# One line of weight loads up to attention, compression chunks in turn with projections, values earlier, taps spread wider

## The chip, the cores and the metric

The kernel runs on one core of a Trainium2 chip. The metric is the device time of one execution in microseconds; the median of several runs is compared.

## What is computed

One layer of a decoder trunk over x of 1024 rows by 1024 columns. All projections of one RMS-normalised input come from one weight matrix: a convolution group (256 channels, gated, causal depthwise filter of 31 taps, LayerNorm, swish) and an attention group (12 query heads, 4 key and value heads of 64) with three branches: compressed blocks, selected blocks and a window. The compressed keys and values come from a small network over windows of 32 rows:

```python
def compress(kr, pe, w1, w2):
    b, t = kr.shape[:2]
    chunks = kr.reshape(b, t // CMP_STRIDE, CMP_STRIDE, N_KV_HEADS, HEAD_DIM)
    lo = jnp.einsum("bclgd,ldh->bcgh", chunks, w1[:CMP_STRIDE])
    hi = jnp.einsum("bclgd,ldh->bcgh", chunks, w1[CMP_STRIDE:])
    h = lo[:, :-1] + hi[:, 1:] + jnp.einsum("ld,ldh->h", pe, w1)
    return jnp.einsum("bngh,hd->bngd", jax.nn.silu(h), w2)
```

The branches are gated and summed, joined with the convolution group, projected out and added to x; a SwiGLU network and a last RMSNorm follow.

## The kernel before

Every product is made of three passes: weights and data are each split into a high part (rounded for the fast matmul type) and a low remainder, and hi·hi, hi·lo and lo·hi are summed in PSUM. A weight chunk therefore costs a load and a split. `load_w` (L214) does it: SP starts the DMA into `w_raw` (two buffers), ACT casts `w_hi` (L225), and POOL subtracts `w_lo` in four pieces (L229), or DVE in one piece where `eng=dve` is given.

```python
raw = wp.tile([P, WCH], F32, tag="raw", name="w_raw", bufs=2)
act.copy(hi[:, :n], raw[:, :n])
step = n // PIECES if eng is pool else n
eng.tensor_sub(lo[:, q], raw[:, q], hi[:, q].bitcast(F32))
```

`w_hi` and `w_lo` have three buffers each. A `Feed` (L193) holds a list of loads and issues each one two ahead of the chunk that is being fetched.

The rows of x are worked on in two halves of 512. The first stretch, up to attention, is written as generators that a `Drive` (L149) runs one after the other on PE: the convolution's input (`conv_in`), the key's rows for the compression (`compress_in`, tiles `zc`, split into `xh` on ACT and `xl` on DVE by L233), the first two query projections (`project_d`, tiles `zo`), the key compression (`compress`: four chunks of w1, 24 matmuls each, into the two banks `h0` and `h1`, then swish, `af` at L475, split `ah`, `al`, and the second matrix in `compress_k`), four more query projections, the window's values (`values`, tiles `vo`), the value's `compress_in`, one window-key and one selected-key projection, the value compression, the two other key projections with `compress_v` (tiles `dup`, `vc`) before the last. Each yields the time it is meant to take; `Drive` adds these up, and side generators that are due are stepped in between: `late_rows` (the second half's rows), `tables`, `taps_in` (the depthwise filter, one DVE instruction per tap, L553), four stages of the compressed branch's scores (`stages_in`: `sc`, `cs`, `pg`, `pt`, `pct`, with an exponential at L623 on ACT), and `conv_tail` (LayerNorm and swish of the filter's result, L567 to L590: `cl`, `cn`, `cm`, `cf`, `m`, then a DMA to `mix_d`). After that, attention takes over, filled by the second half's projections (`fill_b`), whose first is a query projection. A scheduler then fixes the order on each engine; an engine works strictly in that order. In the kernel before, the w1 chunks are loaded inside `compress`, with `w_lo` on DVE, and each group of projections has a feed of its own.

Of the kernel before, what the change touches and what calls it, by code (L numbers as in the profile page):

```python
# [19 lines left out]
P = 128  # L20
# [21 lines left out]
C_KC = C_Q + HEADS * HD  # L42
C_VC = C_KC + 256
# [3 lines left out]
C_VW = C_KW + 256  # L47
# [41 lines left out]
def tile_hymba(ctx: ExitStack, tc, x, attn_norm, w_in, conv_w, conv_b, conv_ln_g, conv_ln_b,  # L89
# [186 lines left out]
    def win_chunk(c0):  # L276
        return load_w([(0, w_in[0, :, c0:c0 + P])], KT, P)
# [66 lines left out]
    def late_rows():  # L344
        for t in range(4, 8):
            with tc.issue_after(rows_in[0].ins), tc.issue_after(rows_in[1].ins):
                late[:] = [norm_rows(xts[t], xts[t], grow, pa, a4("junk"))]
            yield 2.4
            transpose_tile(xts[t], hhi[1], hlo[1], (t % 4) * P)

    rows = a4("rows")[:, :P]
# [76 lines left out]
            for i, z in ((0, zh), (1, zl)):  # L428
                sp.dma_start(dst[i, row:row + P, hf * 512:(hf + 1) * 512], z.bitcast(F32))

    def compress_in(ws, pe_col, out):
        xh = pa.tile([P, 8, GROUPS, 68], F32R, tag="xc", name="xh", bufs=2)
        xl = pa.tile([P, 8, GROUPS, 68], F32R, tag="xc", name="xl", bufs=2)
        for X in (xh, xl):
# [14 lines left out]
                        split(dh, dl, src)  # L449
        out.extend((xh, xl))  # L450

    def compress(xh, xl, w1, w2, tag, out):
        w1f = w1[0].rearrange("l d h -> (l d) h")
        hs = [bank("h0", tag), bank("h1", tag)]
        n = 0
        for jc in range(4):
            wh, wl = load_w([(0, w1f[jc * 512:(jc + 1) * 512, :])], 4, 256, dve)
            if jc == 1:
                w2r = pa.tile([P, 2, HD], F32, tag="w2r", name="w2r")
                pool.tensor_copy(w2r[:, 0, 0:1], wh[:, 0, 0:1].bitcast(F32))  # L460
            for j4 in range(4):
                j, s = (jc * 4 + j4) % 8, jc // 2
                for a, b in ((wh, xh), (wl, xh), (wh, xl)):
                    for ht in range(2):
                        mm(hs[ht][:, :264], a[:, j4, ht * P:(ht + 1) * P], b[:, j, :, s:s + 66],
                           start=n < 2, stop=n >= 94)
                        n += 1
                        yield 0.12
# [391 lines left out]
    def q_load(m):  # L860
        return lambda: win_chunk(C_Q + m * P)
# [16 lines left out]
    def taps_in(n):  # L878
        taps = conv_taps(0)
        for _ in taps:  # L880
            yield n

    drive = Drive()
    xk, xv, kk, kv = [], [], [], []
    turn[1] = ACCS1
    drive.side(late_rows())
    drive.run(conv_in(first, 0))
    drive.side(tables(late[0], 3.0))
    drive.side(taps_in(2.2))
    drive.run(compress_in([win_chunk(C_KC + m * P) for m in range(2)], 68, xk))  # L890
    feed = Feed([q_load(m) for m in range(2)])
    for m in range(2):
        drive.run(project_d(feed, q_d, m * P, (0,), True))
    drive.run(compress(*xk, cmp_k_w1, cmp_k_w2, "s", kk))
    turn[1] = ACCS2
    feed = Feed([q_load(m) for m in range(2, 6)])
    for m in range(2, 6):
        drive.run(project_d(feed, q_d, m * P, (0,), True))
        if m == 2:
            compress_k(*kk)  # L900
            drive.side(stages_in(0), drive.t + 4.0)
        if m == 5:
            drive.side(stages_in(1))
    drive.run(values(Feed(value_loads(C_VW, 18)), 18, vw_d, 0))
    drive.side(stages_in(2))
    drive.run(compress_in([win_chunk(C_VC + m * P) for m in range(2)], 84, xv))
    drive.side(conv_tail(0))
    feed = Feed(kv_loads())
    for dst in (kw_d, ks_d):
        drive.run(project_d(feed, dst, 0, (0,)))  # L910
    drive.side(stages_in(3))
    drive.run(compress(*xv, cmp_v_w1, cmp_v_w2, "z", kv))
    turn[0] = -1
    for dst in (kw_d, ks_d):
        drive.run(project_d(feed, dst, P, (0,)))
        if dst is kw_d:
            compress_v(*kv)
    p2_stack.close()
    pa_stack.close()

# [319 lines left out]
```

## Time and profile before

| | |
|---|---|
| median of 3 runs | 1520.09 us (1519.88 to 1520.77) |
| the profiled execution | 1518.21 us, span 1516.5 us |
| TensorE (PE) busy | 1450.9 us, 96% of the span |
| mean granted TensorE clock | 0.989 of full speed |
| VectorE (DVE), ScalarE (ACT), GpSimd (POOL) busy | 824.9, 721.0, 816.6 us |

PE is the engine that sets the time: idle time of PE, and stretches in which its clock is granted at half, are what a change of order can win or lose. The other engines are each busy about half of the span; they matter where PE waits for them.

### The profile page before, as it was taken

The page shows a single profiled execution, that of the slowest core. Times are in us where ns is not written, and L with a number is a line of the kernel's source. Part 1 is how long each engine was busy: PE and PEld are TensorE (multiplying, and loading weights), DVE is VectorE, ACT ScalarE, POOL GpSimd, SP SyncE. Part 2 cuts the span into 40 slices and gives each one's busy share as a digit, 9 for nine tenths or more (in the row PEclk, how much of TensorE's full clock was granted, in tenths as well). Part 3 has the DMA queues.
Part 4 walks back from the last instruction along what each step waited for, and adds up shares of the span by engine and source line. Part 5 has one row for each costly group of instructions (what it writes and reads, how often), then busy time and mean ns, then how long its engine had stood idle before and what let it go on. Part 6 is the DMA issues. An engine that isn't in the chain of part 4 may idle for free.

```text
span 1516.5 us, 21864 instructions
## 1 busy us (share of the span) xinstructions
PE 1450.9 (96%) x7271; PEld 1217.2 (80%) x7271; DVE 824.9 (54%) x1936; ACT 721.0 (48%) x1468; POOL 816.6 (54%) x1156
## 2 busy tenths in 40 slices
PE   7989989999889889999999999999999999999997
PEld 6778779877768778888888877878788888888886
DVE  6994654667677686776677764223325222222323
ACT  6235655767766476666665654123212222222223
POOL 5626534757576455655664656445532545555554
PEclk9999999999999999999999999999999999999999
DMA  7237567666486362353353225433222322333332
GB/s 239 72 109 209 163 190 213 182 185 190 111 275 181 107 154 76 84 135 92 91 138 97 60 76 171 160 126 104 84 83 97 110 85 89 106 94 93 93 96 84
DMA packets 228717, 193.61 MB, mean 128 GB/s; under 512 B 15496, under 2 KB 197612, under 8 KB 228604
## 3 DMA queue, kind: packets, MB, share of 16 engines
q1 hardware_dynamic: 228604, 192.21, 43.0%
q8 instruction: 58, 0.95, 0.3%
q14 instruction: 55, 0.45, 0.1%
HBM read 158.42 MB, written 33.75 MB: 127 GB/s over the span
## 4 chain that ended last, share of the span: by engine, by line
PE 81%; DVE 7%; DMA 5%; ACT 4%; issue 2%; POOL 1%; SPq 0%; DVEq 0%; POOLq 0%; ACTq 0%
PE gu L1094 31%; PE dn L1114 15%; PE pt L783 5%; PE zo L145 4%; PE wo L1037 3%; PE vo L145 3%; PE wo L1055 3%; DVE cacc L553 3%; PE o L801 3%; DMA w_raw<-in_w_in_dram 2%; PE o L800 2%; PE s L756 2%; PE h L145 2%; DMA mix<-mix_d 1%; PE s L760 1%
## 5 line engine op out<-in xcount | busy, mean ns | idle before, releaser
L229 POOL TENSOR_TENSOR w_lo<-w_raw,w_hi 128x256 fp32r<-128x256 f32 (+1 forms) x688 | 526.8, 800 | 382.8 <-ACT w_hi L225 373.8
L1094 PE MATMUL gu<-h,w_hi 128*128 128x512 f32 x1408 | 454.4, 396 | 0.1
L225 ACT CAST w_hi<-w_raw 128x1024 fp32r<-128x1024 f32 (+1 forms) x182 | 190.4, 1050 | 389.6 <-PE gu L1094 166.9
L1094 PEld LDWEIGHTS gu<-h,w_hi 128*128 128x128 f32 x1408 | 263.1, 188 | 57.7 <-DVE h L233 0.4
L1094 PE MATMUL gu<-h,w_lo 128*128 128x512 f32 x704 | 278.8, 396 | 0.0
L1114 PE MATMUL dn<-w_hi,aw 128*128 128x512 f32 x704 | 234.8, 398 | 4.9 <-DVE af L1101 1.8
L777 POOL TENSOR_SCALAR pr<-pr,l,gates 128x640 f32<-128x640 f32 (+5 forms) x192 | 150.2, 798 | 125.0 <-DVE l L772 97.4
L1101 DVE TENSOR_TENSOR af<-gu,af 128x512 f32<-128x512 f32 x44 | 30.3, 690 | 287.4 <-PE gu L1094 204.9
L767 ACT ACTIVATE pr<-pr,m 128x640 f32<-128x640 f32 (+5 forms) x192 | 141.5, 738 | 93.5 <-DVE m L764 84.3
L1119 DVE TENSOR_TENSOR x<-dn,x 128x512 f32<-128x512 f32 x176 | 114.3, 684 | 94.2 <-PE dn L1114 93.9
L1114 PEld LDWEIGHTS dn<-w_hi,aw 128*128 128x128 f32 x704 | 131.8, 188 | 37.6 <-DVE af L1101 3.3
L233 DVE TENSOR_TENSOR pl<-pt,ph 128x384 fp32r<-128x384 f32 x264 | 141.7, 551 | 37.1 <-ACT ph L233 35.1
L1094 PEld LDWEIGHTS gu<-h,w_lo 128*128 128x128 f32 x704 | 132.2, 188 | 28.8
L233 ACT CAST ph<-pt 128x384 fp32r<-128x384 f32 x264 | 119.3, 478 | 74.6 <-PE pt L783 65.0
L783 PE MATMUL pt<-ident,pr 128*128 128x128 f32 x792 | 135.9, 276 | 3.3 <-DVE pl L233 2.5
L1114 PE MATMUL dn<-w_lo,aw 128*128 128x512 f32 x352 | 138.6, 394 | 0.0
L764 DVE CUSTOM_DVE_ANT_0 pr<-s,base 128x384 f32<-128x384 f32 (+3 forms) x192 | 101.4, 533 | 48.3 <-PE s L760 35.7
L783 PEld LDWEIGHTS pt<-ident,pr 128*128 128x128 f32 x792 | 102.3, 142 | 19.2 <-issue 2.6
L145 PE MATMUL zo<-h,w_hi 128*128 128x512 f32 x320 | 105.8, 400 | 4.0 <-ACT w_hi L225 2.6
L756 PE MATMUL s<-kt,q 128*128 128x384 f32 (+3 forms) x288 | 101.2, 353 | 1.5 <-DVE m L764 0.7
L800 PE MATMUL o<-ph,vt 128*128 128x384 f32 x264 | 98.3, 372 | 1.4 <-ACT ph L233 1.3
L801 PE MATMUL o<-pl,vt 128*128 128x384 f32 x264 | 93.4, 354 | 4.0 <-DVE pl L233 4.0
(207 smaller groups left out, 2320.9 us busy)
## 6 DMA issues: line engine op xcount, KB each, us to landing
w_raw<-in_w_gate_up_dram SPq DMA_DIRECT2D x84, 512.0 KB, 3.9
w_raw<-in_w_down_dram SPq DMA_DIRECT2D x42, 512.0 KB, 3.3
w_raw<-in_w_in_dram SPq DMA_DIRECT2D x40, 512.0 KB, 4.6
mix<-mix_d SPq DMA_DIRECT2D x8, 1024.0 KB, 6.7
q<-q_d SPq DMA_DIRECT2D x80, 96.0 KB, 3.1
qc<-q_d SPq DMA_DIRECT2D x32, 192.0 KB, 4.2
pc_d<-pct SPq DMA_DIRECT2D x16, 384.0 KB, 3.8
pct<-pc_d SPq DMA_DIRECT2D x32, 192.0 KB, 3.4
```

The source lines that it names most:

```text
L145: lastpe[0] = pe.matmul(*args, **kw)
L225: act.copy(hi[:, :n], raw[:, :n])
L229: eng.tensor_sub(lo[:, q], raw[:, q], hi[:, q].bitcast(F32))
L233: return act.copy(hi, src), dve.tensor_sub(lo, src, hi.bitcast(F32))
L756: pe.matmul(sv, q2[:, 0, r, :], kk_[:, 0, kk], start=True, stop=False)
L767: act.activation(pr[:, :n], pr[:, :n], AF.Exp, bias=m, scale=-1.0, accum_out=l3[:, r:r + 1])
L777: pool.tensor_scalar(x_, x_, l3[:, r2:r2 + 1], gates[:, i, c:c + 1], op0=ALU.mult, op1=ALU.mult)
L783: pe.transpose(pt[:, r * P:(r + 1) * P], prs[st][1 + r][:, kk * P:(kk + 1) * P], ident)
L800: pe.matmul(o[:, :384], v, ph, start=False, stop=False)
L801: pe.matmul(o[:, :384], v, pl, start=False, stop=last)
L1094: pe.matmul(o, w[:, k, :], h2[si][h][k // 4][:, k % 4, :], start=n == 0, stop=n == 3 * KT - 1)
L1114: pe.matmul(o, aws[si][:, a, k, t * P:(t + 1) * P], b[:, 0, ch * 512:(ch + 1) * 512], start=n == 0, stop=n == 5)
```

## The change

One feed, `first`, now lists all weight loads up to attention, the eight w1 chunks among them (their `w_lo` is on POOL, in four pieces). The window's values move ahead of the key compression. `in_turn` takes 24 steps of a compression (one chunk), then one whole projection, and so on: four query projections for the key, a selected-key and a window-key projection for the value. The filter's taps come every 2.7 us of `Drive`'s clock where it was 2.2, `late_rows` pauses 4.0 where it was 2.4; `conv_tail` starts 10 us later, the stages of the scores at other points; `compress_v` comes after the last projection. Lines behind L883 are 14 higher in the changed kernel.

```diff
--- before.py
+++ after.py
@@ -345,7 +345,7 @@
         for t in range(4, 8):
             with tc.issue_after(rows_in[0].ins), tc.issue_after(rows_in[1].ins):
                 late[:] = [norm_rows(xts[t], xts[t], grow, pa, a4("junk"))]
-            yield 2.4
+            yield 4.0
             transpose_tile(xts[t], hhi[1], hlo[1], (t % 4) * P)
 
     rows = a4("rows")[:, :P]
@@ -428,7 +428,8 @@
             for i, z in ((0, zh), (1, zl)):
                 sp.dma_start(dst[i, row:row + P, hf * 512:(hf + 1) * 512], z.bitcast(F32))
 
-    def compress_in(ws, pe_col, out):
+    def compress_in(feed, pe_col, out):
+        ws = [feed.get(), feed.get(1)]
         xh = pa.tile([P, 8, GROUPS, 68], F32R, tag="xc", name="xh", bufs=2)
         xl = pa.tile([P, 8, GROUPS, 68], F32R, tag="xc", name="xl", bufs=2)
         for X in (xh, xl):
@@ -449,12 +450,11 @@
                         split(dh, dl, src)
         out.extend((xh, xl))
 
-    def compress(xh, xl, w1, w2, tag, out):
-        w1f = w1[0].rearrange("l d h -> (l d) h")
+    def compress(xh, xl, feed, w2, tag, out):
         hs = [bank("h0", tag), bank("h1", tag)]
         n = 0
         for jc in range(4):
-            wh, wl = load_w([(0, w1f[jc * 512:(jc + 1) * 512, :])], 4, 256, dve)
+            wh, wl = feed.get()
             if jc == 1:
                 w2r = pa.tile([P, 2, HD], F32, tag="w2r", name="w2r")
                 pool.tensor_copy(w2r[:, 0, 0:1], wh[:, 0, 0:1].bitcast(F32))
@@ -880,41 +880,55 @@
         for _ in taps:
             yield n
 
+
+    def in_turn(main, others, part):
+        others = iter(others)
+        for n, d in enumerate(main):
+            yield d
+            if n % part == part - 1:
+                yield from next(others, ())
+        for o in others:
+            yield from o
+
+    def w1_loads(w1):
+        w1f = w1[0].rearrange("l d h -> (l d) h")
+        return [lambda jc=jc: load_w([(0, w1f[jc * 512:(jc + 1) * 512, :])], 4, 256) for jc in range(4)]
+
+    def mixed_in(a, b):
+        return [ld for pair in itertools.zip_longest(a, b) for ld in pair if ld]
+
+    kvl = kv_loads()
+    first.loads += ([lambda m=m: win_chunk(C_KC + m * P) for m in range(2)] + value_loads(C_VW, 18)
+                    + mixed_in(w1_loads(cmp_k_w1), [q_load(m) for m in range(4)]) + [q_load(4), q_load(5)]
+                    + [lambda m=m: win_chunk(C_VC + m * P) for m in range(2)] + kvl[:1]
+                    + mixed_in(w1_loads(cmp_v_w1), kvl[1:3]) + kvl[3:])
     drive = Drive()
     xk, xv, kk, kv = [], [], [], []
     turn[1] = ACCS1
     drive.side(late_rows())
     drive.run(conv_in(first, 0))
     drive.side(tables(late[0], 3.0))
-    drive.side(taps_in(2.2))
-    drive.run(compress_in([win_chunk(C_KC + m * P) for m in range(2)], 68, xk))
-    feed = Feed([q_load(m) for m in range(2)])
-    for m in range(2):
-        drive.run(project_d(feed, q_d, m * P, (0,), True))
-    drive.run(compress(*xk, cmp_k_w1, cmp_k_w2, "s", kk))
+    drive.side(taps_in(2.7))
+    drive.run(compress_in(first, 68, xk))
+    drive.run(values(first, 18, vw_d, 0))
+    drive.run(in_turn(compress(*xk, first, cmp_k_w2, "s", kk),
+                      [project_d(first, q_d, m * P, (0,), True) for m in range(4)], 24))
     turn[1] = ACCS2
-    feed = Feed([q_load(m) for m in range(2, 6)])
-    for m in range(2, 6):
-        drive.run(project_d(feed, q_d, m * P, (0,), True))
-        if m == 2:
-            compress_k(*kk)
-            drive.side(stages_in(0), drive.t + 4.0)
-        if m == 5:
-            drive.side(stages_in(1))
-    drive.run(values(Feed(value_loads(C_VW, 18)), 18, vw_d, 0))
+    drive.run(project_d(first, q_d, 4 * P, (0,), True))
+    compress_k(*kk)
+    drive.side(stages_in(0), drive.t + 4.0)
+    drive.run(project_d(first, q_d, 5 * P, (0,), True))
+    drive.run(compress_in(first, 84, xv))
+    drive.side(stages_in(1))
+    drive.run(project_d(first, kw_d, 0, (0,)))
+    drive.side(conv_tail(0), drive.t + 10.0)
     drive.side(stages_in(2))
-    drive.run(compress_in([win_chunk(C_VC + m * P) for m in range(2)], 84, xv))
-    drive.side(conv_tail(0))
-    feed = Feed(kv_loads())
-    for dst in (kw_d, ks_d):
-        drive.run(project_d(feed, dst, 0, (0,)))
+    turn[1] = "t"
+    drive.run(in_turn(compress(*xv, first, cmp_v_w2, "z", kv),
+                      [project_d(first, dst, r, (0,)) for dst, r in ((ks_d, 0), (kw_d, P))], 24))
     drive.side(stages_in(3))
-    drive.run(compress(*xv, cmp_v_w1, cmp_v_w2, "z", kv))
-    turn[0] = -1
-    for dst in (kw_d, ks_d):
-        drive.run(project_d(feed, dst, P, (0,)))
-        if dst is kw_d:
-            compress_v(*kv)
+    drive.run(project_d(first, ks_d, P, (0,)))
+    compress_v(*kv)
     p2_stack.close()
     pa_stack.close()
 
```

Three places of the order follow, as the program is laid out on the engines, each before and after.

**PE at the first chunk of the key compression.** `zo` is a query projection, `vo` a tile of the window's values, `h0` and `h1` the compression's sums. Before:

```order
L145 MATMUL zo_874<-h0_0_1_128,w_lo_827 128x512
L145 MATMUL zo_874<-h0_1_1_132,w_hi_826 128x512
L145 MATMUL h0_911<-xh_634,w_hi_914 128x264
L145 MATMUL h1_912<-xh_634,w_hi_914 128x264
L145 MATMUL h0_911<-xh_634,w_lo_915 128x264
L145 MATMUL h1_912<-xh_634,w_lo_915 128x264
```

After:

```order
L145 MATMUL vo_912<-w_hi_825,h0_1_1_132 128x274
L145 MATMUL h0_979<-xh_644,w_hi_835 128x264
L145 MATMUL h1_980<-xh_644,w_hi_835 128x264
L145 MATMUL h0_979<-xh_644,w_lo_836 128x264
L145 MATMUL h1_980<-xh_644,w_lo_836 128x264
L145 MATMUL vo_944<-w_hi_635,h0_0_0_127 128x274
L145 MATMUL vo_944<-w_lo_636,h0_0_0_127 128x274
```

Behind the rows of the first fence the 92 other matmuls of the compression follow without a break. In the change four matmuls of the first chunk stand ahead of the fourth value tile, three value tiles stand ahead of them, and the rest of the chunk comes behind that tile.

**DVE while `xl`, the low parts of the compression's input, is made.** `cacc` are the taps; `zl` and `vv` are low parts of a projection and of a value tile. The last `xl` of before is the last row of the first fence, the last of the change the last row of the second.

```order
L425 SCALAR_TENSOR_TENSOR zl_869<-zo_834,qsc_82,zh_868 128x512
L553 SCALAR_TENSOR_TENSOR cacc_646<-y_405,cols_399,cacc_646 128x512
L229 TENSOR_TENSOR w_lo_947<-w_raw_945,w_hi_946 128x1024
L553 SCALAR_TENSOR_TENSOR cacc_647<-y_405,cols_399,cacc_647 128x512
L233 TENSOR_TENSOR xl_635<-zc_776,xh_634 64x8x32
L553 SCALAR_TENSOR_TENSOR cacc_646<-y_405,cols_399,cacc_646 128x512
L233 TENSOR_TENSOR w2l_1060<-w2r_951,w2h_1059 128x2x64 x2
L553 SCALAR_TENSOR_TENSOR cacc_647<-y_405,cols_399,cacc_647 128x512
L233 TENSOR_TENSOR xl_635<-zc_776,xh_634 64x8x32
```

```order
L233 TENSOR_TENSOR xl_645<-zc_784,xh_644 64x8x32
L553 SCALAR_TENSOR_TENSOR cacc_657<-y_405,cols_399,cacc_657 128x512
L233 TENSOR_TENSOR vv_875<-vo_843,vv_875 128x4x64
L298 COPY gates_108<-vo_843 128x18
L553 SCALAR_TENSOR_TENSOR cacc_656<-y_405,cols_399,cacc_656 128x512
L233 TENSOR_TENSOR xl_645<-zc_784,xh_644 64x8x32
L553 SCALAR_TENSOR_TENSOR cacc_657<-y_405,cols_399,cacc_657 128x512
L553 SCALAR_TENSOR_TENSOR cacc_656<-y_405,cols_399,cacc_656 128x512
L233 TENSOR_TENSOR vv_907<-vo_880,vv_907 128x4x64
L298 COPY gates_108<-vo_880 128x18
L233 TENSOR_TENSOR xl_645<-zc_784,xh_644 64x8x32
```

Up to its last `xl`, DVE has 46 taps (L553) before and 42 after; the two weight subtractions L229, one `zl` and the two `w2l` that stood among them are gone, two `vv` and two copies have come.

**ACT and PE at the end of the value compression.** `af` is the swish that frees bank `h0` or `h1`, `cf` and `m2` belong to `conv_tail`, `cs` is the exponential, `zh` the high part of a projection. ACT before:

```order
L225 CAST w_hi_2129<-w_raw_2128 128x1024
L585 ACTIVATE cf_2186<-cm_2183,cols_399 128x128 x2
L233 CAST m2_2189<-cf_2186 128x256
L642 CAST pct_2213<-pt_2214 64x3x128 x2
L225 CAST w_hi_2317<-w_raw_2316 128x1024
L475 ACTIVATE af_2162<-h0_1943,bc_2160 128x256
L233 CAST zh_2230<-zo_2179 128x512
L225 CAST w_hi_2326<-w_raw_2325 128x1024
L233 CAST ah_2158<-af_2162 128x256
L475 ACTIVATE af_2168<-h1_1944,bc_2166 128x256
L233 CAST ah_2158<-af_2168 128x256
L233 CAST zh_2305<-zo_2268 128x512
```

ACT after (the last row is the first `af`):

```order
L233 CAST zh_1982<-zo_1919 128x512
L225 CAST w_hi_1989<-w_raw_1988 128x1024
L585 ACT_TABLE_LOAD
L585 ACTIVATE cf_1953<-cm_1950,cols_399 128x128 x2
L233 CAST m2_1956<-cf_1953 128x256
L623 ACT_TABLE_LOAD
L623 ACTIVATE cs_1929,cl_2030<-cs_1929,bm_2028 128x64 x6
L642 CAST pct_1977<-pt_1978 64x3x128
L225 CAST w_hi_2259<-w_raw_2258 128x1024
L642 CAST pct_1977<-pt_1978 64x3x128
L475 ACT_TABLE_LOAD
L475 ACTIVATE af_2123<-h0_1711,bc_2121 128x256
```

On SP the DMA of `w_raw_2258` stands directly behind that of `m2_1956` to `mix_d`. PE after, where `zo_2286` is the first query projection of the second half and `zo_2140` the last key projection of the first:

```order
L582 MATMUL cm_2077<-ident_75,cn_1973 128x128 x2
L567 MATMUL cl_2090<-ident_75,cacc_656 128x128
L567 MATMUL cl_2090<-ident_75,cacc_657 128x128
L145 MATMUL zo_2286<-h1_129,w_hi_2259 128x512
L145 MATMUL zo_2286<-h1_129,w_lo_2260 128x512
L145 MATMUL zo_2286<-h1_133,w_hi_2259 128x512
L145 MATMUL zo_2286<-h1_129,w_hi_2259 128x512
L145 MATMUL zo_2286<-h1_129,w_lo_2260 128x512
L145 MATMUL zo_2286<-h1_133,w_hi_2259 128x512
L145 MATMUL zo_2286<-h1_129,w_hi_2259 128x512
L145 MATMUL zo_2140<-h0_0_0_127,w_hi_1989 128x512
L145 MATMUL zo_2140<-h0_0_0_127,w_lo_1990 128x512
```

Before, that query projection (`zo_2344`) came behind the last matmul of the key projections; now seven of its matmuls stand ahead of `zo_2140`. The first `af` had no ACT_TABLE_LOAD in front of it before; now there is one. On ACT, the loads of activation tables are 37 in the whole kernel before and 44 after, all seven new ones between the value compression and the start of attention. Later rows of the order (attention, up to the output projection) also differ; the last 1913 instructions of PE are the same.

## Rows read from the trace of the kernel before

**Rows 1.** The page, busy time of each engine.

```profile
PE 1450.9 (96%) x7271; PEld 1217.2 (80%) x7271; DVE 824.9 (54%) x1936; ACT 721.0 (48%) x1468; POOL 816.6 (54%) x1156
```

**Rows 2.** Waits of PE, 0 to 240 us: total, times, longest.

```profile
PE h L145 <- ACT xh L233: 5.1, 1, 5.1
PE h L145 <- ACT w_hi L225: 2.9, 3, 1.6
PE tp L248 <- DVE h L233: 2.9, 1, 2.9
PE h L145 <- DVE w_lo L229: 1.8, 2, 1.0
PE zo L145 <- ACT af L475: 1.4, 1, 1.4
PE h L145 <- DVE crs L573: 0.9, 1, 0.9
...
PE h L145 <- DVE xl L233: 0.5, 1, 0.5
```

**Rows 3.** Stretches: length; PE, PEld, DVE, ACT, POOL busy; clock; DMA share, GB/s.

```profile
96.40:103.40 7.00, 5.94 (x25) 5.64 (x26) 6.17 (x11) 1.99 (x3) 0.00 (x0) 0.51 0.53 176
104.00:112.00 8.00, 8.00 (x66) 8.00 (x65) 7.17 (x8) 2.11 (x3) 2.40 (x3) 1.00 0.70 156
112.40:117.40 5.00, 5.00 (x23) 4.06 (x22) 4.96 (x7) 2.34 (x4) 5.00 (x6) 1.00 0.41 105
...
192.00:195.50 3.50, 3.50 (x18) 3.50 (x18) 0.00 (x0) 0.30 (x1) 0.00 (x0) 0.51 1.01 369
240.00:470.00 230.00, 211.76 (x1205) 182.78 (x1205) 160.79 (x562) 158.72 (x454) 146.69 (x231) 0.98 0.67 193
```

**Rows 4.** Timeline of PE: start, duration, idle before and its releaser.

```profile
96.91 0.81 PE L145 MATMUL h<-xh,w_hi 128*128 128x264 f32 x2 [5.08 <-ACT xh L233]
...
189.13 0.68 PE L145 MATMUL h<-xh,w_hi 128*128 128x264 f32 x2 [1.59 <-ACT w_hi L225]
```

**Rows 5.** Timeline of DVE, near the end of xl.

```profile
92.80 0.74 DVE L425 SCALAR_TENSOR_TENSOR zl<-zo,qsc,zh 128x512 fp32r<-128x512 f32 x1
93.47 0.74 DVE L553 SCALAR_TENSOR_TENSOR cacc<-y,cols,cacc 128x512 f32<-128x512 f32 x1
94.13 1.22 DVE L229 TENSOR_TENSOR w_lo<-w_raw,w_hi 128x1024 fp32r<-128x1024 f32 x1
```

**Rows 6.** Timeline of ACT, near the end of xh, and the first swish of the keys.

```profile
96.49 0.37 ACT L233 CAST xh<-zc 64x256 fp32r<-64x256 f32 x1 [1.76 <-DVE xl L233]
...
113.89 0.48 ACT L475 ACTIVATE af<-h,bc 128x256 f32<-128x256 f32 x1
```

**Rows 7.** Timeline of ACT, 186 to 204 us.

```profile
186.40 0.81 ACT L585 ACTIVATE cf<-cm,cols 128x128 f32<-128x128 f32 x2
187.24 0.40 ACT L233 CAST m<-cf 128x256 fp32r<-128x256 f32 x1
187.55 0.58 ACT L233 CAST zh<-zo 128x512 fp32r<-128x512 f32 x1
...
199.06 0.48 ACT L642 CAST pct<-pt 64x384 fp32r<-64x384 f32 x1
201.39 1.04 ACT L225 CAST w_hi<-w_raw 128x1024 fp32r<-128x1024 f32 x1 [1.85 <-PE h L145]
202.45 1.28 ACT L623 ACT_TABLE_LOAD   x1
203.80 0.35 ACT L623 ACTIVATE cs<-cs,bm 128x64 f32<-128x64 f32 x1
```

**Rows 8.** The page, DMA issues: count, KB, median from issue to landing.

```profile
w_raw<-in_w_in_dram SPq DMA_DIRECT2D x40, 512.0 KB, 4.6
```

**Rows 9.** Timeline of SP, the DMAs of conv_tail's result.

```profile
187.67 1.16 SPq L590 DMA_DIRECT2D mix_d<-m  x2
```

**Rows 10.** Timeline of POOL, w_lo while DVE works taps, and later.

```profile
79.54 5.62 POOL L229 TENSOR_TENSOR w_lo<-w_raw,w_hi 128x256 fp32r<-128x256 f32 x4 [13.15 <-ACT w_hi L225]
...
185.31 2.84 POOL L229 TENSOR_TENSOR w_lo<-w_raw,w_hi 128x256 fp32r<-128x256 f32 x4
```

## The prediction

> **What bounds the kernel now.** I read the page first: PE is busy for 1450.9 of a span of 1516.5 us [rows 1]. The matmuls are the same in both kernels, so no order can win more than the 65 us in which PE is idle, plus what half-clock stretches cost. The waits of PE for the stretch that the change rewrites come next. Its rows [rows 2] are the ceiling of the change: 5.1 + 0.5 us for the key compression's input, 2.9 us for a tile of the second half's rows, and at the value compression 2.9 + 1.8 + 1.4 + 0.9 = 7.0 us, together 15.5 us. The table of stretches adds the clock: 0.51 of full speed, which is the 1.2 GHz level, at 96.4 to 103.4 and 192.0 to 195.5 us [rows 3]. PE had been idle for 5.08 us before the first, and for 1.59 us and once more for 1.0 us shortly before the second [rows 2, 4]. At the full 2.4 GHz a compression matmul takes 8.00/66 = 0.121 us, a projection matmul 5.00/23 = 0.217 us [rows 3]. The 25 matmuls of the first slow stretch would have taken 3.0 us and kept PE busy for 5.94: price 2.9 us. The 18 of the second would have taken 2.2 us and took 3.5: 1.3 us. Attention, which the change reorders without meaning to, has 230.0 - 211.8 = 18.2 us of idle time [rows 3].
>
> **The start, up to the key's rows.** Five more matmuls of the convolution now stand ahead of the second half's transposes, but DVE still makes the split that PE waits for. Of the 2.9 us [rows 2] I give 0.5 to the change, two projection matmuls' worth. The bounds are the whole 2.9, and a loss of 1 us, since the wider pause of `late_rows` delays the same split.
>
> **The key compression.** In the trace PE waits for the last `xh`, cast at 96.49 [rows 6], and starts at 96.91, after 5.08 us of idling from 91.83 [rows 4]. ACT itself waits for DVE there (1.76 us, [rows 6]): DVE works taps between two `xl`. In the change DVE has four taps less up to that point, 4 x 0.74 = 3.0 us, two `w_lo` less, 2.4, and one `zl` less, 0.7 [rows 5]. Two splits of values come in; I price them like `zl`, 1.5. So the last `xh` comes some 4.6 us earlier, at 91.9. PE arrives earlier too: in place of two projections, 48 x 0.217 = 10.4 us, it has three value tiles, which are nearest in size to the compression's matmuls: 72 x 0.121 = 8.7 us. It arrives at 91.83 - 10.4 + 8.7 = 90.1 and waits 1.8 us. The `xl` that follows is covered by the fourth value tile (2.9 us). 5.6 - 1.8 is a gain of **3.8 us** (bounds: 1 if DVE's taps pile up as before, 5.6 if PE doesn't wait at all). A wait of 1.8 us lies nearer to the 1.6 + 1.0 us of the value's place than to 5.08, so I price the clock after it at 1.3 instead of 2.9: **1.6 us** more (0 to 2.9).
>
> **The weights in turn.** With a chunk and a projection in turn PE needs a new load every (24 x 0.121 + 24 x 0.217)/2 = 4.1 us. A load lands in 4.6 us [rows 8], its cast takes 1.04 [rows 7], and POOL's `w_lo` 2.84 [rows 10] where DVE took 1.22 [rows 5]. That is 8.5 us in one of two `w_raw` buffers, one load every 4.2 us. Three buffers of split weights stand ready when the turn begins, so I cost the 0.1 us at **nothing**. The cover is thin: with DVE at its taps the same `w_lo` took 5.62 us [rows 10], and the loads then come every 5.6 us. This is a rival, below. The DVE time set free (eight times 1.22) is off the path, except where counted.
>
> **The value compression.** Its waits, 7.0 us, and 1.3 of the clock go, since the chunks are fetched early: **-8.3 us**. Something new stands at its end. The second half's first query projection uses the bank that `af` frees and is ahead of the last key projection on PE. Its weights come late: on SP their DMA stands behind the DMA of `m2`, and `m2` on ACT behind a weight cast and a table load. From the end of the window-key projection the chain is: cast of `zh` 0.58, cast 1.04, table load 1.28, `cf` 0.81, `m` 0.40 [rows 7], one DMA issue 1.16/2 = 0.58 [rows 9], landing 4.6 [rows 8], cast 1.04, `pct` 0.48, table load 1.28 [rows 7], `af` 0.48 [rows 6]; 12.6 us. PE has two chunks (46 matmuls, the others being ahead) and 23 small ones in that time, 69 x 0.121 = 8.3 us. It idles for **4.3 us** (3 if the load lands as much sooner, 7 if `cf` itself waits for the filter). Such an idle time is nearest to the 5.08, so the clock costs **2.9** (0 to 2.9). What waits behind it on PE is `zo_2140`, which has its weights, and everything after. `vc` waits for the second `af`, which has a table load on each side: 0 to 2.6, I take half, **1.3**. A `pt` waits for one piece of `w_lo` on POOL, 2.84/4 = **0.7**. 9.2 - 8.3: a loss of **0.9 us**, between a gain of 8.3 and a loss of 4.9.
>
> Here a page speaks against the change. The seven added table loads show in the trace as 1.28 us each; the cast in front ends at 202.43, the load begins at 202.45 and ends at 203.73, and the next activation starts at 203.80 [rows 7]. So nothing but the load itself is lost, and I count 1.28. The Trainium skill, "ScalarE: Activation LUTs", section "What ACT_TABLE_LOAD costs", states some 2.66 us for a switch, with a drain of 1.38 us. By it the chain would be 2.8 us longer; the trace here does not show such a drain.
>
> **Attention.** The last stage of the scores runs some 80 PE instructions later, inside attention's start. I cost it and the reordering at 0 +- 3.
>
> **Sum.** -0.5 - 3.8 - 1.6 + 0.9 = -5.0 us. The profiled execution took 1518.21 us, so 1513.2 by its own time; it lies 1.9 below the median, and on the median's scale the changed kernel takes **1515.1 us**. Differences of 0.2%, 3.0 us, are about what a measurement can tell from no change.
>
> **Rivals.**
> - *All waits of the value compression go and none comes*: the bank is free in time because the load lands early. For it: the DMAs of that stretch are few. Against it: the order of SP and ACT. -0.5 - 5.4 - 8.3 = -14.2, **1505.9 us**.
> - *POOL becomes the supply's bound (the slower side)*: `w_lo` at 5.62 us gives a load every (4.6 + 1.04 + 5.62)/2 = 5.6 us against 4.1. The taps now reach deeper into the alternation, and taps are what slowed that row. From 2.6 us of `w_lo` on, every further us costs 0.5 per load. Five loads x 1.5 = 7.5: **1522.6 us**. Against it: at the end of the taps POOL is back at 2.84.
> - *The table loads fall on the path*: seven x 1.28 = 9.0, of which the chain above holds 2.6; 6.4 more makes **1521.5 us**. For it: ACT casts weights, frees banks and feeds the scores in that stretch. Against it: most of the seven stand where PE has a projection to do. The Trainium skill, "ScalarE: Activation LUTs", section on table sets, says to batch the calls by set, which this order does less than before.
> - *What is won is given back in attention*, whose fill, loads and scores take PE's time as they did: **1520.1 us**. For it: 18.2 us of waits there, on many different things. Against it: the work behind is the same whenever it starts.
>
> **How the numbers follow.** Forecast 0.46 (its own range 1511 to 1519.5), first rival 0.17, POOL 0.15, table loads 0.09, given back 0.13. Faster by over 0.2% (under 1517.0): of the forecast 0.33, all of the first, 0.01 of the last: 0.51. Within 0.2%: 0.12 of the forecast, 0.04 of the table loads, 0.10 of the last: 0.26. Slower: 0.01, 0.15, 0.05 and 0.02: 0.23. The range reaches from the first rival, 1505, to beyond the POOL case, 1525; some 0.15 is left out.
>
> **What would show it.** Right: PE's wait for `xh` shrinks to 1 to 3 us and its slow stretch is half as long; the waits for `w_hi` and `w_lo` at the value's chunks are gone; one new wait of `zo` of 3 to 7 us, ended by ACT's `af` or `w_hi`, stands between the value compression and attention, with a slow stretch behind it. Wrong: waits of `h` or `zo` for POOL's `w_lo` between 90 and 135 us (then the POOL case), or no new `zo` wait (then the first rival), or waits of attention that grew by as much as those before it shrank.

## The result and the profile after

The changed kernel takes 1530.11 us in the median of 14 runs, the kernel before 1519.99: ratio 1.0068 (95% interval 1.0047 to 1.0088). It is slower by some 10 us, where 5 us of gain were forecast. The profiled execution took 1526.97 us against 1518.21. It has PE busy for 1455.5 us and idle for 1525.2 - 1455.5 = 69.7 us of its span, against 65.6 [rows 1]:

```profile
PE 1455.5 (95%) x7271; PEld 1214.8 (80%) x7271; DVE 821.5 (54%) x1928; ACT 727.9 (48%) x1475; POOL 840.2 (55%) x1188
```

So 4.1 us of the 8.8 are idle time. Of the 4.6 us that PE is busy for longer, half-clock stretches account for little (34.1 us in this execution against 30.7); the rest I have not traced.

Where the time is lost can be read at a mark that every kernel has, the first matmul of attention (`s`, L756). Before, PE starts it at 239.8 us, and 1276.7 us of the span are left; in the changed kernel it starts at 240.5 us, and 1284.7 are left. Up to the mark the changed kernel has done 16 matmuls more (18 of a value tile at 0.13 us make up most of them), some 2 us by an estimate from these rows. So at equal work it is about 1 us ahead when attention starts, where 5 were forecast, and it loses some 10 us from there on, with less left to do. In the second trace of the same kernel, the control below, the mark is at 243.2 us with 1281.7 left: about 1 us behind at the mark, and a loss of some 7 behind it.

Waits of PE up to 250 us in the changed kernel (total, times, longest), to be laid beside [rows 2]:

```profile
PE tp L248 <- DVE xt L241: 8.1, 1, 8.1
PE cm L582 <- DVE cl L626: 4.3, 1, 4.3
PE tp L248 <- DVE h L233: 2.3, 1, 2.3
PE zo L145 <- ACT af L475: 1.8, 1, 1.8
PE h L145 <- ACT xh L233: 1.8, 1, 1.8
PE vc L506 <- DVE dup L501: 1.6, 2, 1.1
PE s L760 <- DMA kt<-ks_d: 1.1, 1, 1.1
PE vo L145 <- ACT w_hi L225: 0.8, 1, 0.8
PE vo L145 <- DVE gates L298: 0.8, 1, 0.8
PE pt L637 <- POOL pg L631: 0.5, 1, 0.5
```

What the change was made for has happened. The wait for `xh` is 1.8 us in place of 5.1, the waits of the value's chunks for `w_hi` and `w_lo` are gone, and no chunk waits for GpSimd. New are `cm` for DVE (4.3) and `vc` for `dup` (1.6), and `zo` for `af` (1.8) is longer than before: 7.7 us at the end of the value compression, more than the 7.0 that stood there. The text ahead of the prediction places all seven new table loads at this end; the trace has six of them there and the seventh at 98.83 us, for the gates' exponential (L303).

The table of stretches (length; PE, PEld, DVE, ACT, POOL busy; clock; DMA) shows where the idle time lies. Before:

```profile
80.00:180.00 100.00, 94.38 (x514) 81.87 (x513) 68.89 (x145) 48.67 (x130) 48.52 (x63) 0.97 0.58 166
180.00:250.00 70.00, 63.07 (x377) 55.54 (x376) 34.48 (x91) 39.89 (x99) 28.65 (x42) 0.98 0.70 210
250.00:480.00 230.00, 211.76 (x1182) 181.50 (x1181) 162.88 (x559) 159.11 (x447) 145.44 (x225) 0.98 0.64 185
```

After:

```profile
80.00:180.00 100.00, 97.38 (x520) 83.82 (x519) 55.39 (x106) 41.88 (x88) 58.44 (x76) 0.98 0.53 151
180.00:250.00 70.00, 60.55 (x368) 53.36 (x367) 39.07 (x115) 52.54 (x140) 40.19 (x55) 0.93 0.75 220
250.00:480.00 230.00, 207.11 (x1133) 173.94 (x1132) 163.55 (x539) 152.83 (x438) 142.47 (x224) 0.97 0.65 185
```

Idle time of PE falls from 5.6 to 2.6 us in the first stretch, and rises from 6.9 to 9.5 in the second and from 18.2 to 22.9 in the third, which lies in attention. (The stretches are cut at fixed times, so they don't hold quite the same work in both.) The second also has a lower clock, 0.93 against 0.98: from 205.2 to 212.0 and from 225.7 to 229.1 us, 10.2 us together, the granted clock is 0.50, the 1.2 GHz level, in the stretch where PE stood still for 4.28 and 1.80 us and, later, for 1.12 us. Before, there were 3.4 us of it.

In attention one wait stands out that was nearly nothing before: PE's score matmul waits for the running minimum `m` that DVE makes of the scores (L764). Over the whole kernel, before and after:

```profile
PE s L756 <- DVE m L764: 0.7, 3, 0.3
PE s L756 <- DVE m L764: 8.2, 12, 2.8
```

Other waits of attention shrink (`o` for `pl` from 4.0 to 0.9 us), so these 7.5 us are not the loss itself.

How the new wait of 4.3 us comes about is read from three engines. ACT, in the timeline of the changed kernel (start, duration, idle before):

```profile
197.51 1.28 ACT L585 ACT_TABLE_LOAD   x1
198.80 0.81 ACT L585 ACTIVATE cf<-cm,cols 128x128 f32<-128x128 f32 x2
199.65 0.41 ACT L233 CAST m<-cf 128x256 fp32r<-128x256 f32 x1
201.92 1.28 ACT L623 ACT_TABLE_LOAD   x1 [1.87 <-DVE bm L619]
203.22 0.35 ACT L623 ACTIVATE cs<-cs,bm 128x64 f32<-128x64 f32 x1
...
207.17 1.28 ACT L475 ACT_TABLE_LOAD   x1
208.47 0.47 ACT L475 ACTIVATE af<-h,bc 128x256 f32<-128x256 f32 x1
```

DVE:

```profile
200.08 0.94 DVE L233 TENSOR_TENSOR m<-cf,m 128x256 fp32r<-128x256 f32 x1 [2.38 <-ACT m L233]
...
201.68 0.17 DVE L619 TENSOR_TENSOR bm<-cm,slo 128x6 f32<-128x6 f32 x1
205.35 0.17 DVE L625 TENSOR_SCALAR cl<-cl 128x6 f32<-128x6 f32 x1 [3.50 <-ACT cs L623]
205.43 0.54 DVE L576 TENSOR_SCALAR cn<-cl,mv,crs 128x256 f32<-128x256 f32 x1
```

PE:

```profile
206.11 0.66 PE L582 MATMUL cm<-ident,cn 128*128 128x128 f32 x2 [4.28 <-DVE cl L626]
206.56 0.63 PE L567 MATMUL cl<-ident,cacc 128*128 128x128 f32 x2
208.99 0.80 PE L145 MATMUL zo<-h,w_hi 128*128 128x512 f32 x1 [1.80 <-ACT af L475]
```

PE waits for `cn`, the LayerNorm result of the convolution's tail. Its last input, `crs` of GpSimd (L574), is there at 202.35, so DVE could have made it from then on, but it stands behind the score stage's `cl`, which waits for six exponentials on ACT. These wait for a table load, that load waits for `bm` on DVE, and `bm` stands behind `m`, which waited for ACT's swish `cf` and its own table load at 197.51. Two chains, the tail of the convolution and the score stage, step on each other on ACT and on DVE in turn, and each handover on ACT costs a table load.

### The profile page after: what moved, and what is told of

The parts are those of the page before. It is cut to its first block, busy times and chain, and to the rows that moved or that the text cites. A ratio compares the mean times of both kernels' runs of the same rounds, so it can differ in the third digit from the quotient of the medians.

```text
span 1525.2 us, 21887 instructions
## 1 busy us (share of the span) xinstructions
PE 1455.5 (95%) x7271; PEld 1214.8 (80%) x7271; DVE 821.5 (54%) x1928; ACT 727.9 (48%) x1475; POOL 840.2 (55%) x1188
## 4 chain that ended last, share of the span: by engine, by line
PE 71%; DVE 9%; DMA 8%; ACT 4%; issue 4%; POOL 3%; SPq 1%; POOLq 0%; DVEq 0%; ACTq 0%
PE gu L1108 28%; PE dn L1128 15%; PE zo L145 5%; PE pt L783 4%; PE wo L1069 3%; DVE cacc L553 2%; PE wo L1051 2%; PE s L756 2%; PE o L801 2%; DMA w_raw<-in_w_in_dram 2%; PE o L800 2%; POOL w_lo L229 2%; PE zc L145 1%; DMA mix<-mix_d 1%; PE s L760 1%
## 5 line engine op out<-in xcount | busy, mean ns | idle before, releaser
L229 POOL TENSOR_TENSOR w_lo<-w_raw,w_hi 128x256 fp32r<-128x256 f32 (+1 forms) x720 | 552.0, 801 | 366.6 <-ACT w_hi L225 350.4
L783 PEld LDWEIGHTS pt<-ident,pr 128*128 128x128 f32 x792 | 102.8, 141 | 18.2 <-DVE pl L233 1.3
L145 PE MATMUL zo<-h,w_hi 128*128 128x512 f32 x320 | 109.7, 410 | 6.5 <-ACT w_hi L225 4.7
L764 DVE CUSTOM_DVE_ANT_0 pr<-s,base 128x384 f32<-128x384 f32 (+3 forms) x192 | 101.3, 534 | 25.2 <-PE s L760 18.6
L756 PE MATMUL s<-kt,q 128*128 128x384 f32 (+3 forms) x288 | 102.0, 357 | 10.4 <-DVE m L764 8.2
```

The source lines that it names most:

```text
L145: lastpe[0] = pe.matmul(*args, **kw)
L756: pe.matmul(sv, q2[:, 0, r, :], kk_[:, 0, kk], start=True, stop=False)
L783: pe.transpose(pt[:, r * P:(r + 1) * P], prs[st][1 + r][:, kk * P:(kk + 1) * P], ident)
```

## Experiments

Theories: A, the loss arises at the end of the value compression, where swish and exponential alternate; B, the order that attention gets is worse by itself; C, GpSimd's split of w1 limits the supply of weights; D, later, queue order and not the tables. Each kernel was compared with the kernel before on its own chip.

**The key part alone.** The value part is the old one, with the tail of the convolution 8 us later; of the edit, the lines that matter:

```diff
-    drive.run(compress_in(first, 84, xv))
     drive.side(stages_in(1))
...
+    drive.side(conv_tail(0), drive.t + 8.0)
+    feed = Feed(kv_loads())
+    for dst in (kw_d, ks_d):
+        drive.run(project_d(feed, dst, 0, (0,)))
     drive.side(stages_in(3))
...
+    drive.run(compress(*xv, Feed(w1_loads(cmp_v_w1, dve), 1), cmp_v_w2, "z", kv))
```

> Key part as changed (one feed, values ahead, chunks in turn with query projections, taps 2.7, pause 4.0); the value part as before (weights of w1 split on VectorE, all chunks together), with the tail of the convolution 8 us later, since the slower taps are not ready sooner. Theory A (the loss arises at the end of the value compression, where exponentials, swish and their table loads alternate on ScalarE): the 4.5 us won by 186 us stay, the old waits of 7 us at the value's chunks come back, and the time is 1514 to 1517 us, ratio 0.996 to 0.998. Theory B (the reordered attention costs 6 to 10 us by itself, whatever stands ahead): 1521 to 1527. Theory C (GpSimd's split of w1 limits the supply): waits for w_lo in the key part, and no gain.

Measured: 1525.15 us, ratio 1.0033 (1.0015 to 1.0051), above theory A's number and inside theory B's. But by place it is not B's loss: the first matmul of attention starts at 247.1 us, 7.3 later than before, and 1277.2 us are left from there, 0.5 more than before. The loss stands ahead of attention. The waits of PE from 120 to 250 us say why:

```profile
PE pt L637 <- POOL pg L631: 3.8, 2, 2.0
PE h L145 <- ACT w_hi L225: 3.6, 3, 1.3
PE sc L609 <- DMA qc<-q_d: 2.5, 2, 2.3
PE h L145 <- DVE w_lo L229: 1.1, 1, 1.1
```

With the values gone from between them, the score stages come together with the old value chunks: the old waits are back (3.6 + 1.1), and 6.3 us of waits of the stages (`pt`, `sc`) are new. The key part does not stand alone; values ahead with these stages and without the new value part are a loss.

**The value part alone.** The key part is the old one, with its taps at 2.2 and its pause at 2.4; the weights of the value part have a feed of their own, and the tail has no delay. Two of the edits:

```diff
-    drive.run(compress_in(first, 84, xv))
+    drive.run(compress_in(vf, 84, xv))
...
-    drive.side(conv_tail(0), drive.t + 10.0)
+    drive.side(conv_tail(0))
```

> Key part as before, value part as changed (own feed, chunks in turn with key projections, value compression finished after the last projection), tail of the convolution without its delay of 10 us, since the taps are done sooner. From the start of attention its order of instructions is that of the changed kernel. Theory A: the stall at the end of the value compression is there, the 4.5 us of the key part are not: 1531 to 1536 us, ratio 1.007 to 1.011. Theory B: the same number, since the order of attention is the same; then the split by place in the trace decides. Theory C: below 1526, since the key part's supply is the old one.

Measured: 1531.92 us, ratio 1.0085 (1.0066 to 1.0104), as A and B both allow. PE waits 4.7 us for `xh` and 5.2 us for `dup`, which hangs on the second `af`. From the first matmul of attention on, PE's order is row for row that of the changed kernel; ahead of it the value part differs by the places of the tail and of a score stage, and the waits of `cm` and of `zo` for `af` are not there. The mark of attention is at 245.2 us, 5.4 later than before, and 1286.1 us are left, 9.4 more than before. So the larger part of this loss is attention's, theory B. This kernel has 39 table loads, two more than before, and takes as long as the changed kernel with 44: the number of table loads alone can't be the cause. The new key part is not the cause either, and for the key's chunks the supply of theory C is out.

**The tail of the convolution 14 and 18 us later.** One number of the changed kernel:

```diff
-    drive.side(conv_tail(0), drive.t + 10.0)
+    drive.side(conv_tail(0), drive.t + 14.0)
```

> The changed kernel with one number changed: the tail of the convolution starts 14 us later in place of 10. On ScalarE both swishes of the value compression then follow each other with no table load between, and there are 40 table loads in place of 44. Theory A: the waits of 4.3, 1.8 and 1.6 us at the end of the value compression and the half clock behind them shrink to under 3 us together, and the time falls to 1518 to 1523 us, ratio 0.999 to 1.002. Theory B: the order of attention is different again (about 3200 of 5180 rows in common), so anything from 1520 to 1532, and the gain or loss lies inside attention. Theory C: 1530 as before.

Measured: 1518.67 us, ratio 0.9997 (0.9983 to 1.0010), inside theory A's span. PE's waits at the end of the value compression are down to 1.0 us (`pt` for `cf`) and 0.4 us (`dup`).

> The changed kernel with the tail of the convolution 18 us later in place of 10: 38 table loads, and from the start of attention the order of TensorE is row for row that of the run with the changed key part alone. Theory A: key part won, no stall, no old waits at the value's chunks: 1510 to 1515 us, ratio 0.993 to 0.997, which is 4 to 7 below the run with the changed key part alone. Theory B: both runs share what the order of attention costs, so they differ by the value part alone, 4 to 8 us, and both lie above 1518. Theory C: 1527 to 1531.

One statement in this text does not hold: attention's order is not that of the run with the key part alone. In the traces 1160 matmuls stand ahead of attention's first here and 1155 there, and behind it the two orders differ. The comparison of the two is therefore no comparison of the value part alone.

Measured: 1514.85 us, ratio 0.9977 (0.9960 to 0.9994): faster than both kernels. By the ratios, 1.0068 and 0.9977, a delay of 8 us more of one side generator is worth some 14 us. Theory A's number is met, but the order of attention changed with it, so that B is not out. The trace of this kernel is of an execution of 1521.64 us, 6.8 above its median.

**The same order without the table loads.** The exponential of the score stages of the first half becomes an absolute value (the compressed branch of that half is no softmax then):

```diff
-            act.activation(s[:, u, :], s[:, u, :], AF.Exp, scale=-SLOPES[g * REP + u % REP], bias=bm[:, u:u + 1],
+            act.activation(s[:, u, :], s[:, u, :], AF.Abs if qt < 2 else AF.Exp, scale=-SLOPES[g * REP + u % REP], bias=bm[:, u:u + 1],
```

> The changed kernel with the exponential of the score stages of the first half (L623) replaced by an absolute value, which needs no table of its own: ten table loads less (34 in place of 44), and the order of all engines row for row that of the changed kernel. The compressed branch of the first half is then not a softmax. Theory A (table loads at the end of the value compression): the waits of 4.3 and 1.8 us there shrink by the three loads on their chain, 3.8 us, the half clock behind them shortens, and later waits shrink too: 1518 to 1524 us, ratio 0.998 to 1.003. Theory B (the order of attention costs the time by itself): attention's order is untouched, so 1528 to 1531. A third theory, D (the queue order of DVE and ACT costs it, the table loads are only a small part): 1525 to 1528, the wait of cm for cn still over 3 us.

The control, the changed kernel unedited, on the same chip:

> The changed kernel itself, as a control on the same chip as the three others: 1527 to 1533 us, ratio 1.005 to 1.009 by every theory.

Measured: 1522.15 us, ratio 1.0029 (1.0016 to 1.0042), against 1528.76, ratio 1.0065 (1.0048 to 1.0083), for the control. The ten table loads cost 6.6 us by the medians, and the two intervals do not overlap; in the traces every other instruction of PE, ACT, DVE and POOL stands where it stood. This is the price of ten loads and not of the seven new ones: the edit takes away all loads for the exponentials of the first half's score stages, and the kernel before has three of these too (at 132.4, 202.5 and 225.9 us). The traced execution took 1526.82 us, 4.7 above the median, and the control's 1526.55, so their spans don't show the gain. But their order is the same, and between two matmuls it can be read: from the 864th, which belongs to the value compression, to the first of attention PE takes 56.6 us here, 62.1 in the control and 61.6 in the first trace of the changed kernel. The gain, 5.0 to 5.5 us, stands at the end of the value compression. What took it back in this execution lies elsewhere: 1.4 us more than the control in the wait of `tp` for `h` at the start (5.3 against 3.9), and 51.2 us of half clock in all against 41.0.

In this kernel the exponentials follow `bm` without the 1.28 us between, here on ACT:

```profile
205.02 0.35 ACT L623 ACTIVATE cs<-cs,bm 128x64 f32<-128x64 f32 x1 [2.38 <-DVE bm L619]
```

and PE's waits from 180 to 250 us are

```profile
PE zo L145 <- ACT af L475: 2.8, 1, 2.8
PE cm L582 <- DVE cl L626: 0.7, 1, 0.7
```

The wait of `cm` shrank to 0.7 us (2.8 in the control, 4.3 in the first execution), so D, which had it stay over 3, falls. That of `zo` stays, because `w_hi` stands in front of `af` and waits for its DMA, as the prediction had it. The stretches of this kernel:

```profile
180.00:250.00 70.00, 64.69 (x405) 58.14 (x404) 42.05 (x118) 40.68 (x130) 42.52 (x60) 0.95 0.76 229
250.00:480.00 230.00, 208.24 (x1123) 176.36 (x1122) 161.48 (x542) 152.12 (x437) 140.92 (x222) 0.95 0.63 183
```

Idle time from 180 to 250 us is 5.3 us, less than before the change; from 250 to 480 us it is still 21.8. Attention in this order waits as long when the stall ahead of it is small: this part is theory B, and it is 3.6 us more than before. From attention's first matmul 1284.6 us are left, as in the changed kernel (1284.7).

**Tail 17, and the value compression finished earlier.**

> The kernel with the tail 17 us later in place of 18: also 38 table loads, and 5166 of some 5200 rows of attention's order as in the run with 18. Theory A: the same as with 18, 1513 to 1517 us, ratio 0.996 to 0.998. If the time hangs on chance details of the order, it can lie anywhere between 1513 and 1525.

Measured: 1515.24 us, ratio 0.9974 (0.9964 to 0.9985), the same as with 18.

```diff
-    drive.run(project_d(first, ks_d, P, (0,)))
     compress_v(*kv)
+    drive.run(project_d(first, ks_d, P, (0,)))
```

on top of the tail 18 us later:

> The kernel with the tail 18 us later, and the value compression finished ahead of the last key projection, as before the change; from the start of attention its order is that of the run with the tail 18 us later, row for row. Theory A: the wait of vc for dup (1.6 us) and the half clock behind it (10.2 us in that run) shrink: 1511 to 1514 us, ratio 0.993 to 0.996. If the end of the value compression is not what counts any more, 1515.

Measured: 1513.67 us, ratio 0.9966 (0.9954 to 0.9978), and once more on another chip:

> The fastest kernel so far once more, on the chip of the two others: 1511 to 1516 us, ratio 0.995 to 0.998 by every theory.

1516.58 us, ratio 0.9977 (0.9960 to 0.9994). It beats both kernels; that it beats the tail at 18 by itself is not shown, since the intervals overlap. Its wait for `dup` is 1.6 us as in that run (1.3 in the repeat), so this part of the expected reason did not act; the half clock behind it is shorter, 6.8 us and 3.4 in the repeat, for 10.2. ACT in this kernel has one table load for both swishes and `cf`:

```profile
203.78 1.28 ACT L475 ACT_TABLE_LOAD   x1
205.07 0.47 ACT L475 ACTIVATE af<-h,bc 128x256 f32<-128x256 f32 x1
...
209.06 0.47 ACT L475 ACTIVATE af<-h,bc 128x256 f32<-128x256 f32 x1
209.42 0.80 ACT L585 ACTIVATE cf<-cm,cols 128x128 f32<-128x128 f32 x2
```

and its stretches are

```profile
180.00:250.00 70.00, 64.55 (x389) 57.76 (x388) 41.49 (x126) 46.84 (x141) 41.37 (x58) 0.93 0.77 231
250.00:480.00 230.00, 214.23 (x1186) 181.45 (x1184) 164.63 (x561) 160.18 (x448) 148.68 (x231) 0.98 0.66 190
```

5.5 and 15.8 us of idle time (5.5 and 16.7 in the repeat). Against the changed kernel that is 4.0 us less at the end of the value compression and 7.1 less in attention. How much of that is the order's own is uncertain: PE's order from attention's first matmul on is the same in this kernel, its repeat and the tail at 18, and the three traces have 1277.0, 1282.1 and 1284.8 us from there to the end.

**What the key part is worth.** The kernel with the tail at 18 and the old key part, its taps and pause as before; of the edit against the tail at 18:

```diff
-    drive.run(in_turn(compress(*xk, first, cmp_k_w2, "s", kk),
-                      [project_d(first, q_d, m * P, (0,), True) for m in range(4)], 24))
...
+    for m in range(2):
+        drive.run(project_d(feed, q_d, m * P, (0,), True))
+    drive.run(compress(*xk, Feed(w1_loads(cmp_k_w1, dve), 1), cmp_k_w2, "s", kk))
```

> The key part as before the change, the value part of the kernel with the tail 18 us later; attention's order has 4548 of some 5200 rows in common with that kernel. If the changed key part is worth what PE's work against time showed in the traces (4 to 5 us), this kernel takes 1517 to 1521 us, ratio 0.999 to 1.002, and PE's wait for xh is 4.5 to 5.5 us again. If the key part is worth nothing once attention has taken its share, it takes the same as with the new key part, 1513 to 1516, ratio 0.996 to 0.998.

Measured: 1518.21 us, ratio 0.9982 (0.9964 to 1.0000). PE waits 4.8 us for `xh` and 0.5 for `xl` again; 1.7 and 0 with the new key part:

```profile
PE h L145 <- ACT xh L233: 4.8, 1, 4.8
...
PE h L145 <- DVE xl L233: 0.5, 1, 0.5
```

In the time it is not shown: 0.9982 and 0.9977 cannot be told apart, and attention's order differs somewhat as well.

**The split of w1 on VectorE, tail at 18.**

```diff
-                    + mixed_in(w1_loads(cmp_k_w1), [q_load(m) for m in range(4)]) + [q_load(4), q_load(5)])
+                    + mixed_in(w1_loads(cmp_k_w1, dve), [q_load(m) for m in range(4)]) + [q_load(4), q_load(5)])
...
-                    + mixed_in(w1_loads(cmp_v_w1), kvl[1:3]) + kvl[3:])
+                    + mixed_in(w1_loads(cmp_v_w1, dve), kvl[1:3]) + kvl[3:])
```

> The kernel with the tail 18 us later, with the low parts of w1 made by VectorE in one piece, as before the change (POOL 32 instructions less, DVE 8 more). The order is different again and has 42 table loads. Theory C (GpSimd's split limits the supply): the waits for w_hi or w_lo before 200 us, 0.7 us in all with GpSimd, vanish and the time falls below 1513. Otherwise, by theory A, the four added table loads cost 2 to 4 us: 1516 to 1521 us, ratio 0.998 to 1.002.

Measured: 1525.66 us, ratio 1.0042 (1.0025 to 1.0058). Theory C falls: with VectorE the waits for weights are longer, from 80 to 250 us

```profile
PE h L145 <- DVE w_lo L229: 2.0, 1, 2.0
...
PE h L145 <- ACT w_hi L225: 0.7, 1, 0.7
```

The loss is larger than the 2 to 4 us expected for four table loads; the order of attention differs here too, and what each is worth is not separated.

**All traces by place.** The start of attention's first matmul, what is left of the span from there, and PE's idle time from 250 to 480 us; one execution each.

| kernel | attention starts, us | from there to the end | idle, 250 to 480 |
|---|---|---|---|
| before | 239.8 | 1276.7 | 18.2 |
| changed | 240.5 | 1284.7 | 22.9 |
| changed, control | 243.2 | 1281.7 | 20.9 |
| changed, absolute value | 240.5 | 1284.6 | 21.8 |
| value part alone | 245.2 | 1286.1 | 21.6 |
| key part alone | 247.1 | 1277.2 | 16.9 |
| tail 14 | 233.7 | 1283.4 | 18.6 |
| tail 17 | 231.6 | 1281.9 | 19.5 |
| tail 18 | 235.1 | 1284.8 | 18.3 |
| tail 18, finished earlier | 233.3 | 1277.0 | 15.8 |
| the same, repeat | 230.1 | 1282.1 | 16.7 |
| tail 18, old key part | 235.2 | 1282.0 | 17.3 |
| tail 18, w1 on VectorE | 237.2 | 1288.1 | 18.5 |

Two things stand out. The four rows with the changed kernel's order of attention have the four longest idle times there, 20.9 to 22.9 us, whatever stands ahead; this is theory B. And the kernels with the tail at 14 to 18 us start attention 2.6 to 9.6 us earlier than the kernel before, with 5 to 10 matmuls more done, but take as long or longer from there on: against the kernel before, all that they win is won ahead of attention.

## Why the prediction was wrong

- *The start*: 0.5 us expected. The wait went from 2.9 to 2.3 us in the first trace, but it is 3.9 and 5.3 in the two other traces of the same order; a gain is not shown.
- *The key compression*: PE waits 1.8 us, the number forecast, plus 0.8 us that was not seen (a value tile waits for the copy of the gates). The half-clock stretch behind it is 3.4 us long in place of 6.8. 3.1 us of idle time were won for 3.8 forecast. Right.
- *The weights in turn*: costed at nothing, and nothing it is. No chunk waits for `w_lo`; the rival with GpSimd as the bound was wrong.
- *Attention at 0 +- 3*: this step failed, and it holds most of the miss. From its first matmul to the end the changed kernel takes 8.0 us longer in the first trace and 4.9 in the control, with 16 matmuls less to do: 7 to 10 us at equal work. PE's idle time from 250 to 480 us grew by 4.7 and by 2.7 us, and the runs with the same order of attention, no exponentials' table loads or the old key part keep 21.8 and 21.6: the order itself waits more, and it did not come from a late start. The prediction named no row for this term; its only reason, given at the last rival, was that the work behind is the same whenever it starts. The work is, its order is not. Its last sign of being wrong, waits of attention that grow, is what the trace shows. The last rival, a gain given back in attention, had the place right and a chance of 0.13; it stopped at 1520.1 us, and attention took more than the gain.
- *The value compression*: this step failed, too, by size. I had one new idle time of 4.3 us, before `zo_2286`, with `af` behind a weight cast and a table load. The trace has 1.8 us there and 4.3 in front of it, at `cm`, a transpose that I had not followed; that the two numbers are alike is chance. The DMA of the weights, which I had on the chain, landed at 204.85 us, before ACT was done with the exponentials; what held `af` was ACT's own queue. I traced the chain of ACT and SP, and not what stands on DVE behind the score stage's `cl`. With `dup` the idle time is 7.7 us for the forecast's 4.3 + 1.3 + 0.7. The clock term was 2.9: in the 10.2 us at half clock PE is busy for 4.1 + 3.4 us, half of which, 3.7 us, is what it cost. Up to the start of attention the kernel is then about 1 us ahead in one trace and 1 us behind in the other, for 5 us forecast.
- *The table loads*: I held 1.28 us each and the rule to batch calls by set, priced seven loads with 6.4 us beyond the chain, and gave that 0.09. The run puts ten loads at 6.6 us, 0.66 each: about half of what the rival paid for one. That 6.4 and 6.6 are alike is chance, and the rival's time, 1521.5 us, is not what was measured. I held that most of the loads have a projection on PE to hide behind; about half of their 12.8 us was hidden, and the rest stands between two chains that both feed PE.

The Trainium skill, "ScalarE: Activation LUTs", section "Table sets: the hidden batching unit", says to batch activation calls by set; here the measurement bears it out, 6.6 us for ten loads. The same page of the Trainium skill, section "What ACT_TABLE_LOAD costs", gives 2.66 us for a switch; by it ten loads make 26.6 us, an estimate, where the rows' 1.28 us make 12.8. Neither number is the loss; that part of the loads is hidden behind other waits is the likely reason, and no run separates it.

What stays open: which part of attention's new order costs the time. The longest new wait, `s` for `m`, does not decide it, since it is 5.8 to 8.5 us in five traces with the tail at 17 or 18 as well. The changed kernel and the one with the tail at 18 differ by some 14 us; table loads hold at most about 6.6 of it. The rest lies in the order at the end of the value compression and in attention, where the order of several thousand rows moves with every such number, and I have not separated the two further. Also, the run with the key part alone shows that the gain ahead is lost when the score stages meet the old value chunks.

## What to carry to other kernels

When a wait is taken out early in a program, look at what the freed time pushes together: here two side chains that need different activation tables met on ScalarE, and moving one of them by 8 us was worth some 14 us, more than the whole change was forecast to win. Follow each new chain through all queues that it enters, DVE's too, and count what stands in front of each link. Where a scheduler reorders everything behind the change, an unchanged stage is not free: here it held most of the loss. Give it several us on the slow side, compare two kernels at a mark that both have and not only by their waits, and try two or three neighbouring numbers before judging the idea.

## What the runs showed that was not expected

A table load can stand behind its activation's wait. In the changed kernel ACT idles for 1.87 us until DVE's `bm` is done, and only then loads the table (201.92, 1.28 us) and starts the exponentials (203.22). Here the load is thus on the chain of the operand, though the engine had time for it before. It is no rule: in the same trace the load at 929.41 us runs first and ACT then idles for 1.45 us until the operand is there, and in the run of the value part alone an exponential's load at 225.61 us is followed by 1.93 us of waiting for `bm`. What decides between the two is not shown.
